# RWKV-7 loops of a hybrid decoder trunk: the second head pair's keys projected in the first loop's filling, the first pair's last transposes behind them

## The chip, the cores and the metric

The kernel runs on 1 core of one Trainium2 chip. The metric is the device time of one execution in microseconds, the median over several executions. The engines are TensorE (PE in the profile, with PEld for its weight loads), VectorE (DVE), ScalarE (ACT), GpSimd (POOL) and SyncE (SP, which issues most DMAs).

## The reference, cut to what matters

One decoder layer on a sequence of 1024 rows of width 1024: three mixers side by side (HGRN2, dilated window attention, RWKV-7) share one input projection `w_in`; then come an output projection, a gated MLP and an embedding term. The change touches the RWKV-7 mixer and the shared projection that fills its gaps:

```python
r, k, v, wd, ad, gd = jnp.split(cm, splits, axis=-1)      # columns of w_in, mixed with the row before
...
kk = heads(k * k_k)
kk = kk / jnp.maximum(jnp.linalg.norm(kk, axis=-1, keepdims=True), 1e-12)
...
def step(state, inp):
    r_t, w_t, k_t, v_t, kk_t, a_t = inp
    sa = jnp.einsum('bhvk,bhk->bhv', state, -kk_t)
    state = (state * w_t[:, :, None, :] + sa[..., None] * (kk_t * a_t)[:, :, None, :]
             + v_t[..., None] * k_t[:, :, None, :])
    return state, jnp.einsum('bhvk,bhk->bhv', state, r_t)
...
mean = jnp.mean(y, axis=-1, keepdims=True)
var = jnp.mean((y - mean) ** 2, axis=-1, keepdims=True)
y = ((y - mean) * lax.rsqrt(var + RK_GN_EPS)).reshape(B_, S_, RK_WIDTH) * ln_w + ln_b
bonus = jnp.sum(rh * kh * r_k, axis=-1, keepdims=True) * vh
y = (y + bonus.reshape(B_, S_, RK_WIDTH)) * g
```

There are 4 heads of 64, treated as two pairs of 128 channels.

## The kernel before, in words

**The projection and its steps.** `w_in` is cut into column blocks of 128. A block `j` is projected as a product of 1024x128 weights and the 1024x1024 input, in float32 by three passes over split operands: `mm3` runs, for each of 8 slices of the contraction, high by high (L137), low by high (L139) and high by low (L141), two halves of 512 columns each. So a *step* is 6 matmuls into the PSUM tile `dp`, and a block is 8 steps, 48 matmuls. There are 2 dp buffers. The weights come by DMA (`wraw`), are cast to their high part on ScalarE (`whi`, L114) and get their low part on POOL or DVE (`wlo`, L116).

Blocks 0 to 7 are RWKV's own columns (2, 3 and 4 the keys k, receptances r and values v of the first pair, 5, 6 and 7 those of the second); `proj` gives `mix_in` a PSUM tile of one, from `self.early` where it is there already, or by computing it in place. A block's result is scaled on DVE (L320), mixed on ScalarE (L501) and on DVE (L502). Blocks from 8 on belong to the other mixers; they have no place of their own in RWKV, and serve as filling.

**The filling.** `project_rest` is a generator over such blocks: each `next(fill)` issues one step on TensorE. A block's end is drained by `finish` (L454 on DVE for blocks that only need scaling, a scaling L320, ScalarE's L457 and DVE's L459 for the others) into the tile `zst` (2 buffers), which SP stores.

**The order of a pair** (`rwkv`, for p in 0, 1). `rwkv_prep` projects k and r, norms the keys (`kks`, L558, sums of squares; the `lo` matmuls L567 and L570), makes `kkn`, `bhat` and `ar` (L594 to L609) on DVE, issues a count of filling steps, and calls `rwkv_scores` (`sc`, L654, masked on DVE, L656). `rwkv_inverse` then inverts the score tiles by 31 rounds on DVE (L678 and L680, with the end L682), to which DMAs bring and from which they take the matrices (`scz` L664, `At` L670, `Tz` and `Uz` L685, `Tc` L690, `Uc` L695). Over that time 32 filling steps are issued in the first pair, 29 in the second, with the projection of v (in the first pair) and the bonus matmuls `bon` (L635) at fixed steps. `rwkv_main` joins the results (`py`, `pu`, `sk`, all by L790) and runs the groups of the scan with one filling step to a slot; a group's outputs `pyo` and states `pS` come by L790, the state S is updated on DVE (L903), and outputs are added to y (L930). `rwkv_norm` norms a half of 512 columns: mean (`gnm`), variance (`gnv`, L760 and L761), its power on POOL (`gnr`, L763), the product on DVE (L764), four transposes `yt` on TensorE (L770), then L771 to L775 on DVE with the gate `pg` (L774). Half 0 is normed within the loop, half 1 behind it. In the first pair the filling is then drained to its end.

A scheduler of the language orders the instructions of each engine by priorities of the code and its model of when each is ready, and gives a tile the buffer that is free first; a buffer asked for must have been read by all its readers.

Of the kernel before, what the change touches and what calls it, by code (L numbers as in the profile page):

```python
# [18 lines left out]
P = 128  # L19
# [70 lines left out]
class Trunk:  # L90
# [334 lines left out]
    def project_rest(self, js):  # L425


        nc = self.nc
        w = None
        for i, j in enumerate(js):  # L430
            w = w or self.load_w(self.a["w_in"][j])
            ps = self.dps.tile([P, T], F32, tag="dp", name=self.nm("dp"))
            nxt = None
            for k in range(ND):
                self.mm3({0: ps[:, :HT], 1: ps[:, HT:]}, w(k), self.X[k], k == 0, k == ND - 1)
                if k == 3 and i + 1 < len(js):
                    nxt = self.load_w(self.a["w_in"][js[i + 1]])
                yield
            w = nxt
            t = self.keep.tile([P, T], F32, tag="zst", name=self.nm("zst"), bufs=2)  # L440
            kind = (j - 8) % 4 if j < 24 else 2
            parts = [(t, ps, self.R)]
            if j < 24 and kind < 3:
                parts = [(t[:, :HT], ps[:, HT:][:, ::-1], self.R[:, HT:][:, ::-1]), (t[:, HT:], ps[:, :HT], self.R[:, :HT])]
            for part in parts:
                self.finish(kind, *part)
            d = self.zpool.tile([P, T], F32, tag=f"z{j}", name=f"z{j}")
            nc.sync.dma_start(d, t)
            self.z[j] = d
        yield  # L450
# [55 lines left out]
    def rwkv(self):  # L506
        nc, tc = self.nc, self.tc
        lt = self.mix_in(0, 6, "lora")
        nc.scalar.activation(lt[0:64, :], lt[0:64, :], AF.Tanh)
        sg = self.mix_in(1, 7, "sg")  # L510
        nc.scalar.activation(sg, sg, AF.Sigmoid)
        self.z = {}
        js = iter((*range(8, 16), 24, 25, 26, 16, 17, 20, 21, 19, 27, 28, 29, 18, 22, 23))
        for p in (0, 1):
            d = {}
            lead, n = self.FILL[p]
            fill = self.project_rest([next(js) for _ in range(n)])
            with tc.tile_pool(name=f"pre{p}", bufs=1) as tp:
                self.rwkv_prep(p, tp, lt, d, fill)
                self.rwkv_inverse(p, tp, d)  # L520
            for i in range(8 * lead - (3 if p else 8)):
                next(fill)
                if p == 0 and i == 1:
                    d["v"] = self.mix_in(4, 4, "v")
                if i == (7 if p else 16):
                    self.rwkv_bonus(d)
            with tc.tile_pool(name=f"rk{p}", bufs=1) as rp:
                self.rwkv_main(p, rp, sg, d, fill)
            self.rwkv_norm(p, sg, d, 1, fill, 6 - 3 * p)
            if p == 0:  # L530
                for _ in fill:
                    pass
        self.rest, self.more = list(js), fill
# [3 lines left out]
    def rwkv_prep(self, p, tp, lt, d, fill):  # L537

        nc, par = self.nc, self.par
# [24 lines left out]
        for hf in (0, 1):  # L564
            sl = slice(hf * HT, (hf + 1) * HT)
            ps = mxp.tile([P, HT], F32, tag="mx", name=self.nm("lo"))
            nc.tensor.matmul(ps, par[0:64, PC_LORA + p * P:PC_LORA + (p + 1) * P], lt[0:64, sl], start=True, stop=True)  # L567
            nc.scalar.activation(w[:, sl], ps, AF.Sigmoid, bias=col(PC_W0))
            ps = mxp.tile([P, HT], F32, tag="mx", name=self.nm("lo"))
# [39 lines left out]
            nc.vector.tensor_tensor(a4[:, :, :, 1:], k4[:, :, :, 1:], g4[:, :, :, :63], ALU.mult)  # L609
            nc.scalar.copy(a4[:, :, :, 0:1], k4[:, :, :, 0:1])  # L610
        d.update(ar=ar, be=be, kh=kh)
        for _ in range(6 if p else 8):
            next(fill)
        self.rwkv_scores(p, tp, d)
        if p:
# [115 lines left out]
    HALVES = tuple((slice(a, a + 32), slice(a + 32, a + 64)) for a in (0, 64))  # L731

    def rwkv_norm(self, p, sg, d, hf, fill, n):
        for i, _ in enumerate(self.rwkv_norm_steps(p, sg, d, hf)):
            for _ in range(2 if i < 4 else 1):
                for _ in range(1 if n == 3 else 2):
                    next(fill, None)

    def rwkv_norm_steps(self, p, sg, d, hf):

        nc, mxp, par = self.nc, self.mxp, self.par
        y, y3 = d["y"], d["y3"]

        def col(c):
            return par[:, c + p:c + p + 1]

        sl, cs = slice(hf * HT, (hf + 1) * HT), slice(8 * hf, 8 * hf + 8)
        y, y3 = y[:, sl], y3[:, cs, :]
        if hf == 0:
            d["o"] = self.keep.tile([P, T], F32, tag="oc", name=self.nm("oc"), bufs=2)  # L750
        o = d["o"][:, sl]
        mean = self.spool.tile([P, 8], F32, tag="kr1", name=self.nm("gnm"), bufs=1)
        nc.vector.tensor_reduce(mean, y3, AX.X, ALU.add)
        nc.vector.tensor_scalar(mean, mean, 1.0 / 64, None, ALU.mult)
        yield
        nc.vector.tensor_tensor(y3, y3, mean.unsqueeze(2).broadcast_to([P, 8, 64]), ALU.subtract)
        nc.scalar.activation(o, y, AF.Square)
        yield
        var = self.spool.tile([P, 8], F32, tag="kr2", name=self.nm("gnv"), bufs=1)
        nc.vector.tensor_reduce(var, o.rearrange("p (c v) -> p c v", v=64), AX.X, ALU.add)  # L760
        nc.vector.tensor_scalar(var, var, 1.0 / 64, GN_EPS, ALU.mult, ALU.add)  # L761
        rs = self.spool.tile([P, 8], F32, tag="kr3", name=self.nm("gnr"), bufs=1)
        nc.gpsimd.tensor_tensor(rs, var, self.mhalf[:, :8], ALU.pow)  # L763
        nc.vector.tensor_tensor(y3, y3, rs.unsqueeze(2).broadcast_to([P, 8, 64]), ALU.mult)  # L764

        yield
        yield
        pt = mxp.tile([P, HT], F32, tag="mx", name=self.nm("yt"))
        for m in range(4):
            nc.tensor.transpose(self.turned(pt[:, m * P:(m + 1) * P], m % 2), y[:, m * P:(m + 1) * P], self.ident)  # L770
        nc.vector.tensor_scalar(o, pt, col(PC_LNW), col(PC_LNB), ALU.mult, ALU.add)  # L771
        nc.vector.tensor_tensor(o, o, d["bv"][:, sl], ALU.add)
        pg = mxp.tile([P, HT], F32, tag="mx", name=self.nm("pg"))
        nc.tensor.matmul(pg, par[:, PC_G2 + p * P:PC_G2 + (p + 1) * P], sg[:, sl], start=True, stop=True)  # L774
        nc.vector.tensor_tensor(o, o, pg, ALU.mult)  # L775
        if hf:
            self.o[6 + p] = d["o"]
            self.dump(f"o{6 + p}", d["o"])
        yield
# [1080 lines left out]
```

## Time and profile before

| what | us |
|---|---|
| median of 3 runs (1404.64 to 1406.29) | 1404.72 |
| the profiled execution | 1404.77 |
| its span, the first to the last instruction | 1403.0 |
| TensorE busy | 1375.7 |
| VectorE busy | 1063.7 |
| ScalarE busy | 611.8 |
| GpSimd busy | 395.5 |

The profile times are from the start of the span. In a timeline row stand the start, the duration of the whole group, the engine, the line, the operation, what it writes and reads, its size and the number of instructions in the group; in brackets the idle time before it and what released it. The first pair's scores are at 77 us, its norm's transposes at 186 and 199.5 us; the second pair's key sums at 214.7, its scores at 238.6. Matmuls overlap: one begins 0.227 us behind the other and lasts longer.

### The profile page before, as it was taken

The page shows a single profiled execution, that of the slowest core. Times are in us where ns is not written, and L with a number is a line of the kernel's source. Part 1 is how long each engine was busy: PE and PEld are TensorE (multiplying, and loading weights), DVE is VectorE, ACT ScalarE, POOL GpSimd, SP SyncE. Part 2 cuts the span into 40 slices and gives each one's busy share as a digit, 9 for nine tenths or more (in the row PEclk, how much of TensorE's full clock was granted, in tenths as well). Part 3 has the DMA queues.
Part 4 walks back from the last instruction along what each step waited for, and adds up shares of the span by engine and source line. Part 5 has one row for each costly group of instructions (what it writes and reads, how often), then busy time and mean ns, then how long its engine had stood idle before and what let it go on. Part 6 is the DMA issues. An engine that isn't in the chain of part 4 may idle for free.

```text
span 1403.0 us, 22344 instructions
## 1 busy us (share of the span) xinstructions
PE 1375.7 (98%) x8644; PEld 1116.5 (80%) x8644; DVE 1063.7 (76%) x1613; ACT 611.8 (44%) x1049; POOL 395.5 (28%) x287
## 2 busy tenths in 40 slices
PE   9999999999999999999999999999999999999997
PEld 6878777877878768788788888888888888888886
DVE  7696456835667796468889888888988799777685
ACT  7522323133255584255544343444344444455542
POOL 5411012101222242221345454545453000002342
PEclk9999999999999999999999999999999999999998
DMA  6123111321622212653232332332324963441443
GB/s 224 61 83 104 64 61 47 100 73 62 225 83 99 91 61 71 253 180 125 94 127 98 113 103 90 102 105 98 114 98 166 351 217 106 127 143 45 136 138 140
DMA packets 80122, 167.61 MB, mean 119 GB/s; under 512 B 19984, under 2 KB 22288, under 8 KB 80016
## 3 DMA queue, kind: packets, MB, share of 16 engines
q1 hardware_dynamic: 66784, 147.05, 31.3%
q10 hardware_dynamic: 12224, 15.47, 3.2%
q0 software_dynamic: 1008, 3.67, 0.7%
q8 instruction: 68, 1.11, 0.3%
q14 instruction: 38, 0.31, 0.1%
HBM read 119.76 MB, written 46.40 MB: 118 GB/s over the span
## 4 chain that ended last, share of the span: by engine, by line
PE 78%; DVE 8%; issue 8%; ACT 3%; POOL 3%; DMA 1%; SPq 0%; POOLq 0%; ACTq 0%; DVEq 0%
PE bg L1338 17%; PE bv L1338 13%; PE bv L1639 7%; PE bg L1639 7%; PE dp L137 7%; PE dp L139 7%; PE dp L141 7%; PE swq L1169 1%; DVE ig L584 1%; PE hsc L1015 1%; PE zp L137 1%; DVE xl L409 1%; PE zp L141 1%; PE zp L139 1%; PE swo L1209 1%
## 5 line engine op out<-in xcount | busy, mean ns | idle before, releaser
L137 PE MATMUL dp<-xh,whi 128*128 128x512 f32 x544 | 186.9, 406 | 1.2 <-DVE r L502 0.7
L139 PE MATMUL dp<-xl,whi 128*128 128x512 f32 x544 | 180.5, 394 | 0.6 <-DVE xl L409 0.5
L141 PE MATMUL dp<-xh,wlo 128*128 128x512 f32 x544 | 179.7, 392 | 0.0
L116 POOL TENSOR_TENSOR wlo<-wraw,whi 128x512 fp32r<-128x512 f32 x60 | 84.5, 1410 | 264.9 <-ACT whi L114 226.8
L116 POOL TENSOR_TENSOR wlo<-raw,whi 128x512 fp32r<-128x512 f32 x84 | 135.0, 1626 | 75.9 <-ACT whi L114 75.9
L114 ACT CAST whi<-wraw 128x512 fp32r<-128x512 f32 x120 | 72.9, 618 | 158.0 <-PE dp L139 103.0
L1338 PE MATMUL bg<-t,whi 128*128 128x512 f32 x352 | 133.4, 389 | 0.0
L139 PEld LDWEIGHTS dp<-xl,whi 128*128 128x128 f32 x544 | 102.3, 188 | 24.6 <-DVE xl L409 2.5
L141 PEld LDWEIGHTS dp<-xh,wlo 128*128 128x128 f32 x544 | 102.2, 188 | 23.8 <-issue 2.0
L137 PEld LDWEIGHTS dp<-xh,whi 128*128 128x128 f32 x544 | 98.8, 189 | 26.0 <-issue 3.9
L116 POOL TENSOR_TENSOR wlo<-s,whi 128x512 fp32r<-128x512 f32 x44 | 64.5, 1466 | 168.6 <-ACT whi L114 168.6
L1639 PE MATMUL bg<-t,whi 128*128 128x512 f32 x308 | 95.2, 390 | 0.0
L1639 PE MATMUL bv<-t,whi 128*128 128x512 f32 x308 | 94.8, 389 | 0.0
L114 ACT CAST whi<-raw 128x512 fp32r<-128x512 f32 x88 | 52.7, 620 | 93.7 <-issue 48.5
L114 ACT CAST whi<-s 128x512 fp32r<-128x512 f32 x66 | 38.9, 620 | 120.2 <-PE bg L1338 112.8
L1338 PEld LDWEIGHTS bg<-t,whi 128*128 128x128 f32 x352 | 66.1, 188 | 13.7
L190 POOL TENSOR_TENSOR rst<-rst,mhalf 128x4 f32<-128x4 f32 (+1 forms) x9 | 10.2, 1134 | 234.0 <-DVE rst L186 218.0
L1635 ACT CAST t<-t 128x512 fp32r<-128x512 f32 x77 | 47.8, 622 | 45.8 <-PE bv L1639 32.7
L1338 PE MATMUL bg<-t,wlo 128*128 128x512 f32 x176 | 67.5, 389 | 0.0
L1639 PEld LDWEIGHTS bv<-t,whi 128*128 128x128 f32 x308 | 57.8, 188 | 12.0
L1639 PEld LDWEIGHTS bg<-t,whi 128*128 128x128 f32 x308 | 57.8, 188 | 11.9
L116 DVE TENSOR_TENSOR wlo<-wraw,whi 128x512 fp32r<-128x512 f32 x60 | 48.2, 807 | 20.7 <-ACT whi L114 18.5
(417 smaller groups left out, 3423.6 us busy)
## 6 DMA issues: line engine op xcount, KB each, us to landing
raw<-in_ffn_up_dram SPq DMA_DIRECT2D x44, 512.0 KB, 3.5
wraw<-in_w_in_dram SPq DMA_DIRECT2D x28, 512.0 KB, 3.4
z<-zst SPq DMA_DIRECT2D x18, 512.0 KB, 2.9
gb<-ct SPq DMA_DIRECT2D x33, 256.0 KB, 2.3
t<-gb SPq DMA_DIRECT2D x33, 256.0 KB, 2.7
t<-gt SPq DMA_DIRECT2D x33, 256.0 KB, 2.7
zl<-z SPq DMA_DIRECT2D x16, 512.0 KB, 4.4
wraw<-in_ple_gate_dram SPq DMA_DIRECT2D x16, 512.0 KB, 3.4
```

The lines of the kernel that those rows point to most:

```text
L114: self.cast = nc.scalar.copy(hi, src).ins
L116: eng.tensor_tensor(lo, src, hi.bitcast(F32), ALU.subtract)
L137: nc.tensor.matmul(ps[hf], wh, xh[hf], start=first, stop=False)
L139: nc.tensor.matmul(ps[hf], wh, xl[hf], start=False, stop=False)
L141: self.step = nc.tensor.matmul(ps[hf], wl, xh[hf], start=False, stop=last).ins
L409: nc.vector.scalar_tensor_tensor(lo, x, g[:, k:k + 1], hi.bitcast(F32), ALU.mult, ALU.subtract)
L584: nc.vector.reciprocal(ig[:, hf * HT:(hf + 1) * HT], gam[:, hf * HT:(hf + 1) * HT])
L1015: nc.tensor.matmul(sc[g:g + 64, c, :], ks[:, c * P + g:c * P + g + 64], x, start=True, stop=True)
L1169: m = nc.tensor.matmul(pq[h][:, b:b + w], d["q"][hs, qb * P:nk], d["k"][hs, b:b + w], start=True, stop=True)
L1338: nc.tensor.matmul(ps, w[part == 2][:, s], X[k][part == 1], start=start and k == part == 0, stop=k == 3 and part == 2, skip_group_check=no ...
L1635: nc.scalar.copy(xh, x)
L1639: nc.tensor.matmul(ps[m], wt[part == 2][:, m * P:(m + 1) * P], (xh, xl)[part == 1], start=k == part == 0, stop=k == NK - 1 and part == 2)
```

## The change

Four edits. `project_rest` accepts a block below 8: it leaves the result in PSUM under `self.early[j]`, where `proj` finds it, and goes on. The first pair's filling gets block 5 as its last, so the second pair's keys are projected in the steps behind the first loop, and no longer in `rwkv_prep`. `rwkv_prep` issues one more step ahead of the scores (9 instead of 8 in the first pair, 7 instead of 6 in the second). And `rwkv_norm` remembers, in the first pair, the instruction of the fifth step that it issues, and the four transposes of half 1 are issued with an order behind it.

```diff
@@ -437,6 +437,9 @@
                     nxt = self.load_w(self.a["w_in"][js[i + 1]])
                 yield
             w = nxt
+            if j < 8:
+                self.early[j] = ps
+                continue
             t = self.keep.tile([P, T], F32, tag="zst", name=self.nm("zst"), bufs=2)
             kind = (j - 8) % 4 if j < 24 else 2
             parts = [(t, ps, self.R)]
@@ -514,7 +517,7 @@
         for p in (0, 1):
             d = {}
             lead, n = self.FILL[p]
-            fill = self.project_rest([next(js) for _ in range(n)])
+            fill = self.project_rest([next(js) for _ in range(n)] + [5] * (p == 0))
             with tc.tile_pool(name=f"pre{p}", bufs=1) as tp:
                 self.rwkv_prep(p, tp, lt, d, fill)
                 self.rwkv_inverse(p, tp, d)
@@ -609,7 +612,7 @@
             nc.vector.tensor_tensor(a4[:, :, :, 1:], k4[:, :, :, 1:], g4[:, :, :, :63], ALU.mult)
             nc.scalar.copy(a4[:, :, :, 0:1], k4[:, :, :, 0:1])
         d.update(ar=ar, be=be, kh=kh)
-        for _ in range(6 if p else 8):
+        for _ in range(7 if p else 9):
             next(fill)
         self.rwkv_scores(p, tp, d)
         if p:
@@ -731,10 +734,15 @@
     HALVES = tuple((slice(a, a + 32), slice(a + 32, a + 64)) for a in (0, 64))
 
     def rwkv_norm(self, p, sg, d, hf, fill, n):
+        steps = 0
+        self.before = None
         for i, _ in enumerate(self.rwkv_norm_steps(p, sg, d, hf)):
             for _ in range(2 if i < 4 else 1):
                 for _ in range(1 if n == 3 else 2):
                     next(fill, None)
+                    steps += 1
+                    if p == 0 and steps == 5:
+                        self.before = self.step
 
     def rwkv_norm_steps(self, p, sg, d, hf):
 
@@ -766,8 +774,11 @@
         yield
         yield
         pt = mxp.tile([P, HT], F32, tag="mx", name=self.nm("yt"))
-        for m in range(4):
-            nc.tensor.transpose(self.turned(pt[:, m * P:(m + 1) * P], m % 2), y[:, m * P:(m + 1) * P], self.ident)
+        with ExitStack() as order:
+            if hf and self.before:
+                order.enter_context(self.tc.issue_after(self.before))
+            for m in range(4):
+                nc.tensor.transpose(self.turned(pt[:, m * P:(m + 1) * P], m % 2), y[:, m * P:(m + 1) * P], self.ident)
         nc.vector.tensor_scalar(o, pt, col(PC_LNW), col(PC_LNB), ALU.mult, ALU.add)
         nc.vector.tensor_tensor(o, o, d["bv"][:, sl], ALU.add)
         pg = mxp.tile([P, HT], F32, tag="mx", name=self.nm("pg"))
```

The line numbers of the rows below are of each kernel's own: those of the changed kernel are 3 higher from L440 on, 8 higher from L745 on and 11 higher from L769 on. The numbers behind a name count the tiles.

**TensorE, behind the first loop.** dp_334 and dp_330 are block 5, the second pair's keys; yt are the transposes of half 1, pg the gate. Before:

```order
L137 MATMUL dp_334_2067<-xh_3_91,whi_329_2059 128x512
L139 MATMUL dp_334_2067<-xl_20_108,whi_329_2059 128x512
L139 MATMUL dp_334_2067<-xl_4_92,whi_329_2059 128x512
L770 MATMUL yt_325_2044<-cst_76,y_190_1155 128x128
L770 MATMUL yt_325_2044<-cst_76,y_190_1155 128x2x64
L770 MATMUL yt_325_2044<-cst_76,y_190_1155 128x128
L770 MATMUL yt_325_2044<-cst_76,y_190_1155 128x2x64
L774 MATMUL pg_326_2051<-sg_83_458,par_75 128x512
L141 MATMUL dp_334_2067<-xh_19_107,wlo_330_2061 128x512
L141 MATMUL dp_334_2067<-xh_3_91,wlo_330_2061 128x512
L137 MATMUL dp_334_2067<-xh_21_109,whi_329_2059 128x512
```

Now:

```order
L139 MATMUL dp_330_2046<-xl_32_120,whi_320_1961 128x512
L139 MATMUL dp_330_2046<-xl_16_104,whi_320_1961 128x512
L141 MATMUL dp_330_2046<-xh_31_119,wlo_321_1963 128x512
L141 MATMUL dp_330_2046<-xh_15_103,wlo_321_1963 128x512
L781 MATMUL yt_333_2103<-cst_76,y_192_1169 128x128
L781 MATMUL yt_333_2103<-cst_76,y_192_1169 128x2x64
L781 MATMUL yt_333_2103<-cst_76,y_192_1169 128x128
L781 MATMUL yt_333_2103<-cst_76,y_192_1169 128x2x64
L785 MATMUL pg_334_2110<-sg_83_458,par_75 128x512
L137 MATMUL dp_357_2171<-xh_17_105,whi_352_2163 128x512
L137 MATMUL dp_357_2171<-xh_1_89,whi_352_2163 128x512
L139 MATMUL dp_357_2171<-xl_18_106,whi_352_2163 128x512
```

The transposes stood behind the first 10 matmuls of the keys; now all 48 stand ahead of them, and dp_357, block 6 (r), follows. Before, 38 matmuls of the keys and 23 of r came between pg and `kks`; now 18 of r do. From kks to the second pair's scores 71 matmuls of dp stood before, and 72 stand now.

**TensorE, behind the second pair's scores.** dp_392 is v (block 7), dp_372 block 24 and dp_404 block 25, bon the bonus matmuls. Before:

```order
L139 MATMUL dp_372_2263<-xl_32_120,whi_370_2259 128x512
L139 MATMUL dp_372_2263<-xl_16_104,whi_370_2259 128x512
L141 MATMUL dp_372_2263<-xh_31_119,wlo_371_2261 128x512
L141 MATMUL dp_372_2263<-xh_15_103,wlo_371_2261 128x512
L635 MATMUL bon_412_2578<-bv_396_2422,cst_76 128x512
L635 MATMUL bon_413_2581<-bv_396_2422,cst_76 128x512
L137 MATMUL dp_404_2531<-xh_17_105,whi_375_2290 128x512
L137 MATMUL dp_404_2531<-xh_1_89,whi_375_2290 128x512
```

Now:

```order
L139 MATMUL dp_392_2367<-xl_32_120,whi_390_2363 128x512
L139 MATMUL dp_392_2367<-xl_16_104,whi_390_2363 128x512
L141 MATMUL dp_392_2367<-xh_31_119,wlo_391_2365 128x512
L141 MATMUL dp_392_2367<-xh_15_103,wlo_391_2365 128x512
L137 MATMUL dp_372_2263<-xh_31_119,whi_370_2259 128x512
L137 MATMUL dp_372_2263<-xh_15_103,whi_370_2259 128x512
L139 MATMUL dp_372_2263<-xl_32_120,whi_370_2259 128x512
L139 MATMUL dp_372_2263<-xl_16_104,whi_370_2259 128x512
L141 MATMUL dp_372_2263<-xh_31_119,wlo_371_2261 128x512
L141 MATMUL dp_372_2263<-xh_15_103,wlo_371_2261 128x512
L137 MATMUL dp_404_2531<-xh_17_105,whi_375_2290 128x512
L137 MATMUL dp_404_2531<-xh_1_89,whi_375_2290 128x512
```

v's last matmuls stood 12 matmuls ahead of the end of block 24, now 6, and the bonus matmuls, which stood between blocks 24 and 25, now follow 42 matmuls of block 25. In the changed kernel dp_404 has the PSUM buffer of dp_372, in the kernel before that of dp_392.

**VectorE, first norm of the first pair.** gnv is the variance, gnr its power, S the state, zst the drain of a filling block. Before:

```order
L760 TENSOR_REDUCE gnv_311_1926<-oc_297_1824 128x8
L903 SCALAR_TENSOR_TENSOR S_292_1806<-pS_293_1807,gC_135_725,N_274_1662 128x64
L761 TENSOR_SCALAR gnv_311_1926<-gnv_311_1926 128x8
L764 TENSOR_TENSOR y_190_1155<-y_190_1155,gnr_312_1929 128x512
L903 SCALAR_TENSOR_TENSOR S_299_1834<-pS_300_1835,gC_135_725,N_274_1662 128x64
L116 TENSOR_TENSOR wlo_356_2169<-wraw_350_2161,whi_355_2167 128x512
```

Now:

```order
L768 TENSOR_REDUCE gnv_311_1932<-oc_297_1830 128x8
L914 SCALAR_TENSOR_TENSOR S_292_1812<-pS_293_1813,gC_137_739,N_274_1668 128x64
L457 TENSOR_TENSOR zst_299_1834<-dp_237_1474,rstd_121 128x512 x2
L769 TENSOR_SCALAR gnv_311_1932<-gnv_311_1932 128x8
L772 TENSOR_TENSOR y_192_1169<-y_192_1169,gnr_312_1935 128x512
L914 SCALAR_TENSOR_TENSOR S_301_1846<-pS_302_1847,gC_137_739,N_274_1668 128x64
```

A drain of two instructions (dp_237, block 14 of the filling) now stands between the variance's sum and its scaling; before, it stood five rows further on. On GpSimd the row behind this gnr is now a weight's low part, `wlo_321`, where a memset (`Uc_402`) stood before.

In the first pair the scores keep their place on TensorE. Behind them stood 39 matmuls of block 9, the bonus and 48 matmuls of v; now come 12 of block 9, 48 of v and 27 of block 9, the bonus 108 rows later, and `py` one step later. On VectorE v's L320 now stands ahead of the first L678 and L502 behind the third; on ScalarE three casts of weights stand ahead of v's L501; on SP the store of block 8 and a weight load stand ahead of the `At` copies. From the middle of the second loop on the two orders agree on TensorE.

## Prediction

> **What bounds the kernel now.** First the page: the busy times, and the chain that ended last.
>
> ```profile
> PE 1375.7 (98%) x8644; PEld 1116.5 (80%) x8644; DVE 1063.7 (76%) x1613; ACT 611.8 (44%) x1049; POOL 395.5 (28%) x287
> ```
>
> TensorE is busy 1375.7 of 1403.0 us. The change adds and removes no matmul, so only TensorE's 27.3 us of idle time can change. The table by windows gives the idle time of the stretch that is edited (columns: window, its length, then PE, PEld, DVE, ACT and POOL busy, clock, DMA share, GB/s):
>
> ```profile
> 60.00:100.00 40.00, 39.03 (x249) 31.25 (x249) 36.30 (x53) 8.98 (x16) 10.06 (x7) 1.00 0.26 86
> 130.00:175.00 45.00, 44.35 (x770) 34.20 (x769) 19.37 (x58) 18.46 (x51) 3.86 (x3) 1.00 0.21 73
> 215.00:240.00 25.00, 23.61 (x190) 18.17 (x189) 18.72 (x17) 9.07 (x13) 5.07 (x3) 1.00 0.06 22
> 275.00:330.00 55.00, 54.52 (x776) 42.35 (x774) 24.38 (x66) 19.16 (x51) 2.58 (x2) 1.00 0.24 69
> ```
>
> Idle: 0.97, 0.65, 1.39 and 0.48, and between them, at 199 us, one wait of 1.65 whose row follows below: together 5.14 us. That is all that the edits can win here. TensorE's waits name the other causes (in all, times, longest):
>
> ```profile
> PE sc L654 <- DVE ar L609: 1.4, 2, 0.8
> PE dp L137 <- DVE r L502: 0.7, 1, 0.7
> PE sk L790 <- DVE S L903: 0.6, 1, 0.6
> ```
>
> The sum is made against the profiled execution, 1404.77 us (span 1403.0 and 1.77 around it), 0.05 above the median of 1404.72. It takes 0.2%, 2.8 us, to tell a change of this kernel from none.
>
> **The transposes of y (edit 4): −1.65.** TensorE's timeline, with the last join of the first pair and the transposes; then two steps of a projection:
>
> ```profile
> 190.30 0.34 PE L790 MATMUL pyo<-S,MG 64*64 64x64 f32 x8
> ...
> 197.25 0.61 PE L139 MATMUL dp<-xl,whi 128*128 128x512 f32 x2
> 199.52 0.63 PE L770 MATMUL yt<-cst,y 128*128 128x128 f32 x4 [1.65 <-DVE y L764]
> 199.98 1.02 PE L774 MATMUL pg<-sg,par 128*128 128x512 f32 x2
> 200.44 1.02 PE L141 MATMUL dp<-xh,wlo 128*128 128x512 f32 x2
> ...
> 209.05 0.62 PE L141 MATMUL dp<-xh,wlo 128*128 128x512 f32 x2
> ...
> 210.41 0.62 PE L141 MATMUL dp<-xh,wlo 128*128 128x512 f32 x2
> ```
>
> Six matmuls, a step, take 210.41 − 209.05 = 1.36 us, 0.227 each. The y chain takes from 190.30 to 199.52, 9.2 us. Before, 28 matmuls (18 and 10) and the pyo block stood in front of the transposes; now 60 do (12 and 48), 13.6 us. The wait of 1.65 ends with 4 us to spare.
>
> **The second pair's scores (edits 2 and 3): −0.23.** The scores wait for `ar`, a chain that begins with `kks`:
>
> ```profile
> 214.72 1.87 PE L558 MATMUL kks<-few,kksq 128*128 128x2 f32 x16
> ...
> 238.55 1.52 PE L654 MATMUL sc<-ar,bhat 64*64 64x64 f32 x64 [0.56 <-DVE ar L609]
> ```
>
> From kks to scores are 23.83 us, in which TensorE idles 1.39 (0.7 for r, 0.56 for the scores and 0.13 smaller). The matmuls of dp between them were 71 (25, 36, 10), and are 72 (30, 42): the step "more" is nearly used up because kks now comes sooner behind the keys' last matmul. One row more covers 0.23 and leaves 1.16, under whichever name.
>
> **The keys' own chain: +0.4.** Behind the keys' last matmul stood 23 matmuls (5.21 us) ahead of kks; now stand the transposes, pg (200.44 − 199.52 = 0.92) and 18 matmuls (4.08): 5.00. What must fit there is this:
>
> ```profile
> 209.70 1.23 DVE L320 TENSOR_TENSOR dp<-dp,rstd 128x1024 f32<-128x1024 f32 x1 [4.55 <-PE dp L141]
> 212.12 1.28 DVE L502 SCALAR_TENSOR_TENSOR k<-dp,par,k 128x1023 f32<-128x1023 f32 x1 [1.19 <-ACT k L501]
> ...
> 200.42 0.80 DVE L771 TENSOR_SCALAR oc<-yt,par 128x512 f32<-128x512 f32 x1
> 201.26 0.69 DVE L772 TENSOR_TENSOR oc<-oc,bv 128x512 f32<-128x512 f32 x1
> ```
>
> ```profile
> 213.44 1.15 ACT L555 ACTIVATE kksq<-k,par 128x1024 f32<-128x1024 f32 x1 [1.35 <-DVE k L502]
> ```
>
> The squares end at 214.59, 0.13 before kks. Now L771 and L772, 1.49 us, stand on DVE between L320 and L502, where 1.19 were idle: +0.30. The chain needs 5.21 − 0.13 + 0.30 = 5.4 and has 5.0: a wait of 0.4 (bounds 0 and 0.5).
>
> **A new wait for a drain: +1.55.** A projection takes one of two dp buffers. Before, the projection of column block 25 (L137) followed the bonus matmuls:
>
> ```profile
> 251.51 1.96 PE L635 MATMUL bon<-bv,cst 128*128 128x512 f32 x4
> ```
>
> ```profile
> 197.63 1.74 DVE L764 TENSOR_TENSOR y<-y,gnr 128x512 f32<-128x512 f32 x1 [0.56 <-POOL gnr L763]
> ...
> 248.95 1.23 DVE L320 TENSOR_TENSOR dp<-dp,rstd 128x1024 f32<-128x1024 f32 x1 [5.60 <-PE dp L141]
> ...
> 252.57 1.21 DVE L454 TENSOR_TENSOR zst<-dp,rstd 128x1024 f32<-128x1024 f32 x1
> ```
>
> Before, v ended two steps (12 matmuls) ahead of block 24, and block 25 took v's buffer after the bonus. Now v ends one step ahead of 24, the bonus has moved 42 matmuls back, and block 25 takes the buffer of 24, whose only reader is L454. DVE begins 0.19 behind a block's last matmul (the keys' ended at 214.72 − 5.21 = 209.51, L320 began at 209.70). L320 of v takes 1.23 of the step of 1.36, so L454 begins 0.19 behind block 24's last matmul and lasts 1.21. From the end of a DVE row to TensorE's next were 0.15 (L764 ended at 197.63 + 1.74 = 199.37, the transposes began at 199.52). Block 25 waits 0.19 + 1.21 + 0.15 = 1.55 (bounds 1.3 and 1.7). The later of two nearly simultaneous ends is drained with nothing of TensorE's beside it. The Trainium skill ("Perfetto Trace Analysis", section "Matmuls") says that independent groups should rotate through PSUM banks so that draining one overlaps the next group's matmuls. Block 25 breaks that rule here; by the rule the price is a whole drain, 1.21 by the row above, and the sum 0.34 lower.
>
> **The end of the first loop: +0.5.** DVE's rows at the first pair's first norm, POOL's beside its second (whose L764 is shown above), and the join on TensorE:
>
> ```profile
> 178.91 0.69 DVE L764 TENSOR_TENSOR y<-y,gnr 128x512 f32<-128x512 f32 x1 [1.76 <-POOL gnr L763]
> 179.52 0.28 DVE L903 SCALAR_TENSOR_TENSOR S<-pS,gC,N 128x64 f32<-128x64 f32 x1
> ...
> 181.80 1.28 DVE L454 TENSOR_TENSOR zst<-dp,rstd 128x512 f32<-128x512 f32 x2
> ```
>
> ```profile
> 197.56 1.27 POOL L116 TENSOR_TENSOR wlo<-wraw,whi 128x512 fp32r<-128x512 f32 x1
> ```
>
> ```profile
> 181.38 0.34 PE L790 MATMUL pyo<-S,MG 64*64 64x64 f32 x8
> ```
>
> Two things now delay the first norm's L764 and with it the state update L903 behind it: the two L454 stand ahead of gnv (L761), 1.28 us, and POOL starts a wlo right behind gnr, as it did in the second norm, where L764 took 1.74 instead of 0.69: +1.05. Together 2.3. From L903's end (179.80) to the pyo that reads S (181.38) are 1.58: pyo would wait 0.7. DVE idled 1.76 just there before, and part of an L454 may fit into such a gap, so I take 0.5 (bounds 0 and 1.1). The Trainium skill ("SBUF — State Buffer", section "Who interferes with whom") says that a VectorE instruction with two SBUF inputs against a GpSimd one that reads SBUF blocks for the whole instruction, whoever issues first winning. That speaks against this change: by it L764 would last 1.27 − 0.07 + 0.69 = 1.9, an estimate from its rule and these rows, and the term would be 0.15 larger. The 1.74 measured is near it.
>
> **Smaller terms: −0.3 and −0.4.** The `sk` wait on S (0.65, the idle time of the window 130 to 175) comes from S queued on DVE behind a projection's drain; the drains come one step earlier now. Bounds −0.65 and 0; I take the half, −0.3. In the second pair's join TensorE idles 0.48, mostly for the inverse's transposed blocks Tc; the join comes later by the drain's wait and 10 matmuls, and the inverse on DVE by under a us: −0.4 (bounds −0.48 and 0).
>
> **Costed at nothing.** The first pair's scores have the same matmul places: their wait stays.
>
> ```profile
> 77.00 1.52 PE L654 MATMUL sc<-ar,bhat 64*64 64x64 f32 x64 [0.83 <-DVE ar L609]
> ```
>
> Behind them v is projected at once, and on DVE its L320 (1.23) goes ahead of the inverse (L678), whose first row was ready at 89.61:
>
> ```profile
> 89.61 1.29 DVE L678 TENSOR_TENSOR Tt<-At,Tb 64x31 f32<-64x31 f32 x1
> ...
> 122.61 1.12 DVE L682 COPY Ub<-Tb 64x1024 f32<-64x1024 f32 x1
> ```
>
> ```profile
> 132.82 1.20 PE L790 MATMUL py<-Tc,sc 32*32 32x32 f32 x64
> ```
>
> v ends 60 matmuls behind the scores, at 78.5 + 13.6 = 92.1, L320 at 93.5: the inverse starts 3.9 later, and one L320 of the same shape, 1.2, that stood inside it goes, so it ends 2.7 later. py is 1.36 later. In the first pair 10.2 us lie between L682 and py with no wait, in which the Tc copies go out. The tile's own rows give their first and last start, and the time to landing:
>
> ```profile
> L690 SPq DMA_DIRECT2D Tc<-Tz x4: 334/510/682, 125.6 to 127.2; - x4
> ...
> DMA to landing us min/median/max: 1.9/2.9/4.1
> ```
>
> The last is issued at 127.2 and lands 1.9 to 4.1 later, so 1.5 to 3.7 are spare ahead of py, and 1.36 more: 2.9 at least against 2.7. Hidden, just; bounds 0 and +0.5. SP's queue, which the z store of block 8 and one weight load now pass ahead of the At copies, lies in the same slack.
>
> **Sum.** −1.65 − 0.23 + 0.4 + 1.55 + 0.5 − 0.3 − 0.4 = −0.13: 1404.77 − 0.13 = 1404.6 us. An exchange of waits.
>
> **Rivals.** *Faster:* the two new waits and the keys' one don't appear, because DVE runs L454 in a gap. Then −0.13 − 2.45 = −2.58: 1402.2; and if the scores' 1.16 goes too, 1401.0. For it: DVE is idle often. Against it: L454 cannot start before the last matmul of its block. *Slower:* the first pair's v is held on ScalarE. Casts of weights now stand ahead of v's activation (L501):
>
> ```profile
> 94.39 0.62 ACT L114 CAST whi<-wraw 128x512 fp32r<-128x512 f32 x1 [2.25 <-PE dp L139]
> ...
> 103.58 1.12 ACT L501 ACTIVATE v<-dp,omm 128x1024 f32<-128x1024 f32 x1 [3.06 <-DVE dp L320]
> ```
>
> A cast waits for TensorE to release a weight buffer. If they wait for the second weight half of block 9, last read about 85 matmuls behind the scores (97.8), v is ready at 97.8 + 2 × 0.62 + 1.12 = 100.2 instead of 94.6, and DVE's L502, queued three rows into the inverse, holds it 5.6 longer. With 2.7 that is 8.3 against a slack of 2.9 to 5.1: about 4.3 over, 1408.9. It decides above a hold of about 2. Against it: the buffers that those casts take were read by the weights before. *The moved tail:* L771, L772 and L775 (2.2 us) lie wholly on the keys' chain, not 0.3 of them: 1404.6 + 1.9 = 1406.5. Against it: DVE is idle for r's and k's activations there. *It does not do what it says:* the step ahead of scores is already one row in my sum, so this is no case of its own.
>
> **How the numbers follow.** Exchange 0.60, faster 0.20 (half of it, 0.11 with the tails of the others, beyond 2.8 us), moved tail 0.11, slower 0.09. The exchange's own bounds, few of them at once, give about 1403.2 to 1406.0. The range takes in the first step of the faster rival and the moved tail: 1402.2 to 1406.9. Faster by over 0.2% 0.11, within 0.80, slower 0.09.
>
> **What would show it.** Right: no wait at yt; block 25's first L137 waits about 1.55 for L454; a pyo in the first loop's last group waits for S; the second scores wait in all about 1.2; kks waits a few tenths. Wrong: block 25 starts at once, or py of the first pair waits for Tc, or a wait above 1 us anywhere else before 420 us.

## The result and the profile after

| | before | changed |
|---|---|---|
| median of 22 runs, us | 1405.73 (1403.96 to 1406.87) | 1407.92 (1405.47 to 1409.55) |
| ratio, 95% interval | | 1.0013 (1.0007 to 1.0019) |
| profiled execution, us (span) | 1404.77 (1403.0) | 1406.55 (1404.7) |

The change costs 1.8 us (1.0 to 2.7) by the ratio, which goes by the means, 1405.63 and 1407.49; the medians lie 2.2 apart. That is under the 0.2% named in the prediction, and it is clear of zero: not an exchange of waits, as predicted, but a small loss.

TensorE's waits in the changed kernel between 60 and 420 us (in all, times, longest) show that most of the named waits went as predicted:

```profile
PE sc L657 <- DVE ar L612: 2.4, 3, 1.3
PE dp L137 <- DVE zst L457: 1.3, 1, 1.3
PE sk L801 <- DVE S L914: 0.6, 1, 0.6
PE pyo L801 <- DVE S L914: 0.4, 1, 0.4
```

The transposes no longer appear. The projection of block 25 waits for the drain of block 24, and a pyo waits for the state, both forecast. The same in TensorE's timeline:

```profile
184.01 0.33 PE L801 MATMUL pyo<-S,MG 64*64 64x64 f32 x4
184.73 0.27 PE L801 MATMUL pyo<-S,MG 64*64 64x64 f32 x2 [0.39 <-DVE S L914]
...
208.74 0.60 PE L781 MATMUL yt<-cst,y 128*128 128x128 f32 x4
...
214.14 1.84 PE L561 MATMUL kks<-few,kksq 128*128 128x2 f32 x16
...
237.89 0.34 PE L657 MATMUL sc<-ar,bhat 64*64 64x64 f32 x8 [1.30 <-DVE ar L612]
238.48 1.04 PE L657 MATMUL sc<-ar,bhat 64*64 64x64 f32 x56 [0.25 <-DVE ar L612]
...
253.32 0.74 PE L137 MATMUL dp<-xh,whi 128*128 128x512 f32 x2 [1.32 <-DVE zst L457]
```

The transposes begin with no wait; kks follows them by 5.40 us with no wait; the scores still wait, now in two pieces, 1.30 and 0.25. By windows (PE busy of each window's length):

```profile
130.00:175.00 45.00, 44.92 (x753) 1.00 0.27 78
175.00:200.00 25.00, 24.40 (x288) 1.00 0.19 66
215.00:240.00 25.00, 23.45 (x187) 1.00 0.07 23
252.00:275.00 23.00, 21.68 (x92) 1.00 0.27 92
275.00:330.00 55.00, 54.86 (x723) 1.00 0.26 69
330.00:345.00 15.00, 14.25 (x262) 1.00 0.31 107
```

The idle times are 0.08, 0.60, 1.55, 1.32, 0.14 and 0.75, with 0.98 in 60 to 100 5.4 us, as before. And yet the stretch is longer. A wait that the profile brackets is shorter than what it costs: a projection matmul starts 0.227 behind the one ahead but is drawn 0.39 long, and the end drawn hides the first part of every stall. For block 25 the bracket says 1.32, while from the start of block 24's last matmul to the start of its own are 1.70, a stall of 1.47. A break within a join can carry no bracket at all, as that of the first pair's does (below).

A count without this fault compares the starts of the same matmul in both traces and takes off 0.227 for each projection matmul more or less ahead of it. Against the first profile of before the changed kernel loses 0.25 behind the first scores, 0.5 in the first pair's join and 1.1 at the end of the first loop; it wins 0.6 at the first loop's sk and 1.8 at the transposes; it wins 0.2 up to the second scores, loses 1.6 up to the bonus matmuls, wins 0.6 at the second join, and loses 0.4 in the second loop: 0.8 in all, before the parts are rounded. Behind the loops 0.9 more is lost; that is under e5.

### The profile page after: what moved, and what is told of

It reads as the page before. It is cut to its first block, busy times and chain, and to the rows that moved or that the text cites. A ratio compares the mean times of both kernels' runs of the same rounds, so it can differ in the third digit from the quotient of the medians.

```text
span 1404.7 us, 22342 instructions
## 1 busy us (share of the span) xinstructions
PE 1375.7 (98%) x8644; PEld 1116.1 (79%) x8644; DVE 1060.9 (76%) x1613; ACT 612.2 (44%) x1049; POOL 394.5 (28%) x287
## 4 chain that ended last, share of the span: by engine, by line
PE 81%; DVE 9%; issue 3%; ACT 2%; POOL 2%; DMA 2%; SPq 0%; POOLq 0%; ACTq 0%; DVEq 0%
PE bg L1349 17%; PE bv L1349 13%; PE bv L1650 7%; PE bg L1650 7%; PE dp L137 7%; PE dp L139 7%; PE dp L141 7%; PE swq L1180 1%; PE hsc L1026 1%; DVE ig L587 1%; DVE Tt L681 1%; PE zp L137 1%; PE swt L1206 1%; PE swo L1220 1%; PE zp L141 1%
## 5 line engine op out<-in xcount | busy, mean ns | idle before, releaser
L1647 DVE TENSOR_TENSOR t<-t,t 128x512 fp32r<-128x512 f32 x77 | 55.0, 714 | 9.0 <-ACT t L1646 8.7
```

Source lines behind the costliest of these rows:

```text
L1647: V.tensor_tensor(xl, x, xh.bitcast(F32), ALU.subtract)
```

## The experiments

Each stands against runs of the kernel before on the same chip; microseconds are the ratio times 1405. The last column comes from the profiles alone: the time from the first pair's scores to the row of `swd` (L204, a matmul of another mixer at 463 us, behind both loops), less the 385.7 that the two profiles of before took (385.78 and 385.65; the changed kernel 386.56, e4 386.49). Two profiles of the same order differ by about 0.1 there, where a ratio is uncertain by 0.8 to 1.7 us. It leaves out the start, and what comes behind 463 us. The row of swd in the first profile of before and in the changed kernel (the scores of these two begin at 77.00 and 78.01):

```profile
462.78 1.09 PE L204 MATMUL swd<-cst,sden 128*64 128x128 f32 x16
```

```profile
464.57 1.09 PE L204 MATMUL swd<-cst,sden 128*64 128x128 f32 x16
```

| kernel | steps ahead of scores | keys in the filling | ratio (95%) | us | scores to `swd`, us |
|---|---|---|---|---|---|
| changed | 9, 7 | yes | 1.0013 (1.0007 to 1.0019) | +1.8 | +0.8 |
| e4, edit 4 undone | 9, 7 | yes | 1.0014 (1.0005 to 1.0023) | +2.0 | +0.8 |
| e1 | 8, 7 | yes | 0.9999 (0.9991 to 1.0008) | −0.1 | −0.6 |
| e2 | 9, 6 | yes | 0.9993 (0.9984 to 1.0002) | −1.0 | −1.1 |
| e8 | 8, 6 | yes | 0.9982 (0.9973 to 0.9991) | −2.5 | −2.6 |
| e3 | 8, 8 | yes | 0.9971 (0.9959 to 0.9983) | −4.1 | −3.7 |
| e10 | 9, 8 | yes | 0.9982 (0.9973 to 0.9991) | −2.5 | −3.2 |
| e11 | 8, 9 | yes | 0.9966 (0.9954 to 0.9978) | −4.8 | −3.6 |
| e9, low parts on DVE | 9, 7 | yes | 1.0001 (0.9992 to 1.0010) | +0.1 | +0.2 |
| e7 | 9, 7 | no | 1.0018 (1.0009 to 1.0027) | +2.5 | +2.3 |
| e6 | 8, 8 | no | 0.9992 (0.9983 to 1.0001) | −1.1 | −1.5 |
| e5, before again | 8, 6 | no | 1.0002 (0.9993 to 1.0012) | +0.3 | −0.1 |

**e4: the order of the transposes taken away.**

```diff
-            if hf and self.before:
+            if False:
                 order.enter_context(self.tc.issue_after(self.before))
```

> The changed kernel without edit 4 (the transposes have no order behind the fifth step). The order of the instructions on every engine is then the same as in the changed kernel, so edit 4 decides nothing once the keys are in the filling, and this run is a second look at the changed kernel: +1.8 against the kernel before within 0.6. It tells what of the first profile is not of the change: if the inputs at the start land as late as there (+1.2 at 20 us against the kernel before) the start is part of the change, if not it is scatter of one execution.

Measured +2.0 with the same waits in the same places. The order of instructions on all engines is the same without edit 4: once the keys are in the filling, their 48 matmuls stand ahead of the transposes anyway. Edit 4 does nothing.

**e5: the kernel before, a second profile.**

> The kernel before, unchanged, as a second profile of it. All five profiles with the change have the first matmuls 0.9 to 1.4 us later at 20 us than the one profile of before, though the program is the same up to there. If that is scatter of one execution, this profile is late too, by about 1; if it is due to the change, this profile is as the first. Times: 0 within 0.7.

The first pair's scores, ahead of which the programs issue the same, in the changed kernel, in e5, in e1 and in e10:

```profile
78.01 1.52 PE L657 MATMUL sc<-ar,bhat 64*64 64x64 f32 x64 [0.85 <-DVE ar L612]
```

```profile
77.75 1.52 PE L654 MATMUL sc<-ar,bhat 64*64 64x64 f32 x64 [0.83 <-DVE ar L609]
```

```profile
78.37 1.52 PE L657 MATMUL sc<-ar,bhat 64*64 64x64 f32 x64 [0.82 <-DVE ar L612]
```

```profile
77.24 1.52 PE L657 MATMUL sc<-ar,bhat 64*64 64x64 f32 x64 [0.82 <-DVE ar L612]
```

Before had 77.00. The unchanged program has 77.75 here, and among all profiles they lie between 77.0 and 78.4 with no relation to the change. The start is scatter, and the first profile of before was a lucky one there. So the rival "the loss is at the start" falls, though 1.0 of the 1.7 between the first two spans does come from there.

Behind 500 us the first profile was unlucky: TensorE was granted half its clock for some 3.4 us at 511 us (0.50 in the window 511.4 to 514.7), in e5, the changed kernel and e4 not. The first profile of before, e5 and the changed kernel (the column behind PE's is the granted clock):

```profile
500.00:520.00 20.00, 17.56 (x138) 0.91 0.14 41
500.00:520.00 20.00, 17.61 (x167) 1.00 0.14 42
500.00:520.00 20.00, 17.57 (x163) 1.00 0.21 63
```

From swd to the last matmuls (`bv`, L196) the first profile took 933.2 and e5 932.2, so the half clock cost 1.0, and only e5 is a fair measure of what lies behind it. The changed kernel took 932.6, e4 932.5, 0.3 more than e5: at 538 us `vt` waits 1.46 for DVE's `ho`, in e5 1.18. From bv to the end of the span both took 7.6, and e5 7.0. With the 0.8 up to swd this makes 1.7 to 1.8, the time that was measured. The 0.8 is the one counted place by place above. Why the 0.9 behind it is lost is open; e9, with the same steps and keys, has neither part (932.2 and 7.0), so it need not come from the change.

**e1, e2 and e8: one step ahead of the scores undone, then both.**

```diff
-        for _ in range(7 if p else 9):
+        for _ in range(7 if p else 8):     # e1
+        for _ in range(6 if p else 9):     # e2
+        for _ in range(6 if p else 8):     # e8
```

> The changed kernel with the first pair's step ahead of scores undone (8 and 7 instead of 9 and 7). Theory: the changed kernel loses 1.8 us to the one before. Its own profile shows +1.5 for the drain of block 24, -1.8 for the transposes, -0.6 in the second pair's join, and in the first pair +0.4 in the join and +1.1 at the outputs of the last group of the first loop, -0.6 at sk. If the last three come from the first pair's extra step, this run is 0.9 faster than the changed kernel, so about +0.9 against the kernel before, and the wait for block 24's drain stays at 1.3 to 1.6. Rival: the 1.8 come from the start of the program (inputs landing 1 us later in the profile of after) or from the stretch behind 420 us, and then this run is at +1.8 within 0.5, like every other kernel with the change.

> The changed kernel with the second pair's step ahead of scores undone (9 and 6). Theory: the bonus matmuls stand between blocks 24 and 25 again and block 25 no longer waits for the drain of block 24 (-1.5), but the second scores come a step earlier and wait about 1.4 more: near the changed kernel, +1.8 against the kernel before, within 0.5. The wait of dp for zst is gone and that of sc for ar is about 3. Rival: the drain's wait is paid elsewhere anyway and the step is pure gain: this run is 1.4 slower than the changed kernel, +3.2.

> The changed kernel with both steps undone (8 and 6): the keys in the filling alone. Theory: the transposes' wait goes (-1.65), block 25 stands behind the bonus matmuls and waits for no drain, the scores of the second pair wait as long as before or 0.5 less: -1.9 against the kernel before by the profiles, -3 if the times of the runs with one step undone add up. Rival: the saved wait comes back at the second scores, which hang on the keys: 0.

Both steps cost: −0.1 and −1.0 against the +1.8 of the changed kernel, so e1 gains 1.9 where I expected 0.9. Without either the kernel is 2.5 faster than before, between the 1.9 and the 3 expected. The costs add up: by the times the first pair's ninth step costs 1.9 (e1 to the changed kernel) and 1.5 (e8 to e2), the second pair's seventh 2.4 (e8 to e1) and 2.8 (e2 to the changed kernel), each uncertain by 1.5 to 1.8. The profiles up to swd give 1.45 twice for the ninth step and 2.0 twice for the seventh. My expectation for e2 was wrong by nearly 3 us: I held that the scores would wait 1.4 more with a step less. TensorE in e2:

```profile
214.18 1.85 PE L561 MATMUL kks<-few,kksq 128*128 128x2 f32 x16
...
237.93 1.52 PE L657 MATMUL sc<-ar,bhat 64*64 64x64 f32 x64 [1.33 <-DVE ar L612]
...
252.27 1.96 PE L638 MATMUL bon<-bv,cst 128*128 128x512 f32 x4
```

From kks to scores are 23.75 us in e2, and 23.75 in the changed kernel, and the wait is 1.33 against 1.30. The step did not come ahead of the scores at all: with 6 steps the scheduler puts 5 matmuls of v there instead, 71 in place of 72. What the step does is to shift block 24 by six matmuls against v, and with it the drain: in e2 and e8 block 25 follows the bonus matmuls and waits for nothing. With the wait of sk for S in the second loop (idle in 330 to 345: 0.75 in the changed kernel, 0.20 in e2) the drain's 1.47 makes 2.0, the step's cost by the profiles. The break of 0.25 in the scores costs 0.1 from start to start.

The idle time of e1 at the end of the first loop and in the second:

```profile
175.00:200.00 25.00, 25.00 (x284) 1.00 0.19 66
...
252.00:275.00 23.00, 22.77 (x96) 1.00 0.26 92
...
330.00:345.00 15.00, 14.27 (x264) 1.00 0.30 107
```

With 8 steps in the first pair no pyo waits (25.00 busy); the second pair's sk keeps its 0.73. (The window 252 to 275 cuts block 25's wait at its start, in e1 at 250.9.)

**e3: a step more in the second pair, not less.**

```diff
-        for _ in range(7 if p else 9):
+        for _ in range(8):
```

> The changed kernel with 8 steps ahead of the scores in both pairs (instead of 9 and 7). In the second pair block 24 then ends ahead of the scores and is drained beside them, and v's 48 matmuls come between it and block 25. Theory: no wait of dp for zst (-1.5), the second scores wait 0.2 to 0.3 instead of 1.6 (-1.3), and the first pair is as in the kernel with 8 and 7 (-0.9): together -3.7 against the changed kernel, about -1.9 against the kernel before. Rival: the later scores make the second inverse late and the time comes back at the join: py waits 1.4 for Tc, and the run is at -0.5 against the kernel before. Rival of the place: the 1.8 don't come from this stretch, and the run is at -1.0 or above.

Measured −4.1, which is 5.9 below the changed kernel where 3.7 were expected: the direction and the place are right, and both steps cost more than the profiles' rows had told. To swd it is 4.5 below the changed kernel. The windows of e3:

```profile
215.00:240.00 25.00, 24.75 (x190) 1.00 0.07 23
252.00:275.00 23.00, 23.00 (x100) 1.00 0.18 67
275.00:330.00 55.00, 54.92 (x797) 1.00 0.26 78
```

78 matmuls cover the second scores, whose wait falls from 1.55 to 0.25; block 24 ends ahead of them and its drain has v's 48 matmuls beside it; and the join waits for nothing, so the time does not come back there. The saved us stay saved.

**e10 and e11: 9 and 8, 8 and 9.**

> The changed kernel with 9 and 8 steps. Theory: the first pair's ninth step costs by itself, in its join and in its last group, whatever the second pair does: 1.4 to 2.0 more than with 8 and 8, so about -2.4 against the kernel before. Rival: it costs only beside the second pair's 7: as with 8 and 8, -4.1.

> The changed kernel with 8 and 9 steps: six more matmuls of a further block ahead of the second scores. Theory: with 8 the scores have 0.25 of wait left, so a ninth step gains 0.25 at most, and it puts one step of block 25 ahead of v, so that v ends with block 25 half open: the next block waits for v's buffer, whose last reader is v's L505, 1.2 to 2.5 of new wait: -2 to -3 against the kernel before. Rival: more steps ahead of the scores are better still: below -4.1.

e10 lands on its number, −2.5, but does not show what it was made for: the 1.6 by which it stands above e3 are uncertain by 2.1, and to swd the two profiles differ by 0.5 alone. The ninth step costs 1.5 there up to the second scores, but e3 gives most of the rest back in the second loop, where TensorE idles 0.40 between 330 and 345 us in e3 and not at all in e10. e11 was forecast wrongly. The wait that I named, of a block for v's buffer, does not appear; another does, v itself waits for block 24's drain behind the scores:

```profile
237.17 1.16 PE L657 MATMUL sc<-ar,bhat 64*64 64x64 f32 x64
239.85 0.74 PE L137 MATMUL dp<-xh,whi 128*128 128x512 f32 x2 [1.52 <-DVE zst L457]
```

That 1.5 takes what the ninth step wins at the scores and further on, and e11 and e3 are equal: within their intervals, and to 0.1 at swd. Both are faster than the kernel before and the changed one.

**e6 and e7: the steps without the keys.** The kernel before with the counts of e3, and of the changed kernel.

```diff
-        for _ in range(6 if p else 8):
+        for _ in range(8):                 # e6
+        for _ in range(7 if p else 9):     # e7
```

> The kernel before with 8 steps ahead of the scores in both pairs, and the keys not in the filling. Theory: the transposes wait their 1.65 again and r its 0.7, the second scores are covered by 73 matmuls instead of 71 (-0.45), no drain is waited for, and the join comes later (-0.5): -1.0 against the kernel before. Against the kernel with the change and 8 and 8 (measured at -4.1) that is +3. Rival: the two steps are what made that kernel fast and the keys in the filling are worth nothing: this run is at -3 to -4.

> The kernel before with edit 3 alone (9 and 7). Theory: the first pair's step costs 1.4 to 2 and the second pair's 1.6 to 2.9, as between the runs before, and the transposes still wait 1.65, less 0.9 for four matmuls more ahead of them: together +2 to +4 against the kernel before, slower than the changed kernel. Rival: the steps cost only together with the keys in the filling: 0.

Both as expected, −1.1 and +2.5. The keys in the filling are worth 2.5 with 8 and 6 steps, 3.0 with 8 and 8, but 0.7 with 9 and 7 by the times; 2.6, 2.2 and 1.4 by the profiles up to swd. With 9 and 7 the first loop's end lies in the way: from start to start it costs e7 0.4 and the changed kernel 1.1. In e7 no low part stands on POOL behind gnr, the first norm's product takes 0.69, and no pyo waits for S, though the two drains stand ahead of gnv there as well. The transposes wait 1.5 again, and the drain's wait is there too. DVE at the first norm, then TensorE:

```profile
179.12 1.28 DVE L454 TENSOR_TENSOR zst<-dp,rstd 128x512 f32<-128x512 f32 x2
180.32 0.16 DVE L761 TENSOR_SCALAR gnv<-gnv 128x8 f32<-128x8 f32 x1
...
182.61 0.69 DVE L764 TENSOR_TENSOR y<-y,gnr 128x512 f32<-128x512 f32 x1 [1.53 <-POOL gnr L763]
```

```profile
201.54 0.63 PE L770 MATMUL yt<-cst,y 128*128 128x128 f32 x4 [1.54 <-DVE y L764]
...
239.67 1.52 PE L654 MATMUL sc<-ar,bhat 64*64 64x64 f32 x64 [1.61 <-DVE ar L609]
254.06 0.72 PE L137 MATMUL dp<-xh,whi 128*128 128x512 f32 x2 [1.32 <-DVE zst L454]
```

**e9: no low part on POOL behind the first norm.** The low parts of the weights of blocks 5 and 6 are all made on DVE.

```diff
-    def load_w(self, src):
+    def load_w(self, src, own=None):
...
-            parts.append(self.split2(raw[:, b * HT:(b + 1) * HT], self.nc.gpsimd if self.uid % 2 else self.nc.vector))
+            parts.append(self.split2(raw[:, b * HT:(b + 1) * HT], own or (self.nc.gpsimd if self.uid % 2 else self.nc.vector)))
...
-                    nxt = self.load_w(self.a["w_in"][js[i + 1]])
+                    nxt = self.load_w(self.a["w_in"][js[i + 1]], nc.vector if js[i + 1] == 5 else None)
...
-            w = self.load_w(self.a["w_in"][j])
+            w = self.load_w(self.a["w_in"][j], self.nc.vector if j == 6 else None)
```

> The changed kernel with the low parts of the weights of blocks 5 and 6 all made on VectorE, so that no low part follows the first norm's gnr on POOL; on TensorE the order stays. Theory: the product of the norm on DVE lasts 0.69 instead of 1.77 there, the state update behind it comes 1.1 earlier, and the outputs of the last group no longer wait for it (0.4 and the 0.2 behind it): the profile loses 0.6 to 1.0 in that place, against the changed kernel, at about +1.0 against the kernel before. Rival: the two drains ahead of gnv are the delay that counts, and DVE's two low parts more take the place of the hold: the wait for S stays over 0.3 and the time at +1.8.

DVE and POOL at the first norm in the changed kernel:

```profile
179.40 0.28 DVE L914 SCALAR_TENSOR_TENSOR S<-pS,gC,N 128x64 f32<-128x64 f32 x1
179.59 1.28 DVE L457 TENSOR_TENSOR zst<-dp,rstd 128x512 f32<-128x512 f32 x2
180.79 0.16 DVE L769 TENSOR_SCALAR gnv<-gnv 128x8 f32<-128x8 f32 x1
182.71 1.77 DVE L772 TENSOR_TENSOR y<-y,gnr 128x512 f32<-128x512 f32 x1 [1.76 <-POOL gnr L771]
184.41 0.27 DVE L914 SCALAR_TENSOR_TENSOR S<-pS,gC,N 128x64 f32<-128x64 f32 x1
```

```profile
181.03 1.64 POOL L771 TENSOR_TENSOR gnr<-gnv,mhalf 128x8 f32<-128x8 f32 x1 [0.18 <-DVE gnv L769]
182.63 2.98 POOL L116 TENSOR_TENSOR wlo<-wraw,whi 128x512 fp32r<-128x512 f32 x2
```

And DVE in e9:

```profile
182.21 0.69 DVE L772 TENSOR_TENSOR y<-y,gnr 128x512 f32<-128x512 f32 x1 [1.76 <-POOL gnr L771]
182.82 0.28 DVE L914 SCALAR_TENSOR_TENSOR S<-pS,gC,N 128x64 f32<-128x64 f32 x1
...
184.50 1.88 DVE L116 TENSOR_TENSOR wlo<-wraw,whi 128x512 fp32r<-128x512 f32 x3
```

The product takes 0.69 instead of 1.77, the state comes 1.1 earlier behind it, and the pyo's wait is gone. In its place pS waits 0.5 for the next state, so that of the 1.1 only 0.5 is left at the transposes, start to start: half of the rival came true. To swd e9 is 0.7 below the changed kernel. The time is +0.1, 1.7 below it; the two intervals allow 0.2 to 3.2. The hold by POOL is shown, and its worth in the time is 0.7 by the profile, by the times only its sign.

## Why the prediction was wrong

The forecast was −0.1 and 1404.6; measured are +1.8 and 1407.9. 1.0 of the miss in the absolute time is the kernel before itself: 22 runs of it have a median of 1405.73, where the three that the forecast started from had 1404.72. The rest is the sum, step by step:

- *The transposes, −1.65:* right. No wait, −1.8 from start to start. But it was put down to edit 4, and that edit is inert (e4): the keys in the filling do it.
- *The second scores, −0.23:* the reasoning was right that the step is nearly used up, and the wait stayed: idle 1.39 before, 1.55 after in that window. Start to start it is −0.2. The cover was never the point of that step, as e2 shows.
- *The keys' own chain, +0.4:* wrong, 0. I took 0.92 for the transposes and pg from the starts of grouped rows; from the transposes to kks are 5.40, where I had 5.00. The chain of 5.4 just fits.
- *The drain of block 24, +1.55:* right, 1.47 from start to start. e2, e8 and e3 take it away, in two different ways.
- *The end of the first loop, +0.5:* right in mechanism, and too small: 1.1. L772 took 1.77, as the second norm's row had told, and all of the two drains' 1.28 lay ahead of it; no gap took them up. The working gave 0.7 and I cut it to 0.5. pyo's break, 0.2 for MG and a broken order of pyo and pS stand behind it. The Trainium skill's rule ("SBUF — State Buffer", section "Who interferes with whom"), by which the forecast estimated 1.9, is near the 1.77: POOL began at 182.63, DVE at 182.71, and without POOL's row the same instruction took 0.69 (e9, and e7).
- *sk, −0.3:* the wait in the first loop went (−0.6), but the same wait came in the second loop, 0.4 to 0.55: sum near 0. The second loop's filling is shifted by the second pair's step in the same way, and I did not carry the reason over to it. In e1 both loops have it, in e2 neither.
- *The second join, −0.4:* right, −0.6.
- *The first join, costed at nothing:* wrong, +0.5. I looked for Tc to be late, and Tc was not. TensorE in the changed kernel, then ScalarE in the kernel before and in the changed one:

```profile
139.02 0.24 PE L801 MATMUL pu<-Uc,Y 32*32 32x32 f32 x2
139.19 0.44 PE L801 MATMUL sk<-ar,khat 64*64 64x128 f32 x4
139.56 1.19 PE L801 MATMUL pu<-Uc,Y 32*32 32x32 f32 x62
```

```profile
135.76 0.58 ACT L720 COPY Y<-py 32x512 f32<-32x512 f32 x1
136.36 0.60 ACT L457 ACTIVATE zst<-dp 128x512 f32<-128x512 f32 x1
```

```profile
138.28 0.62 ACT L460 ACTIVATE zst<-dp 128x512 f32<-128x512 f32 x1
138.92 0.58 ACT L723 COPY Y<-py 32x512 f32<-32x512 f32 x1
```

The filling's drain, shifted by the step, stood behind the second copy of Y on ScalarE and now stands ahead of it; pu begins, breaks and goes on when Y is whole. No wait is bracketed, since sk's matmuls fill part of the break.

With the measured sizes the sum is −1.8 − 0.2 + 0 + 1.6 + 1.1 − 0.6 + 0.4 − 0.6 + 0.5 + 0.25 = +0.65, or +0.8 before rounding, as counted directly up to swd. The 0.25 is at v's projection behind the first scores, and was not in the forecast; in e1, e3 and e8, without the ninth step, it is not there. The rest up to 1.8 are the 0.9 behind swd, of which only the place is known (e5), and where the forecast had priced nothing.

Of the rivals, *slower* was named with the wrong mechanism: v was not held on ScalarE, its activation began at 94.96, 0.04 behind L320's end. The moved tail of the norm cost nothing.

The failed step of the working is the price of the first pair's ninth step. The forecast put it at +0.5 at the end of the loop and −0.3 at sk, +0.2 in all; it measured +1.45 up to swd (e1 to the changed kernel). Three sizes were wrong: the end of the first loop cost 1.1 for 0.5, the first join 0.5 where only Tc had been looked at, and v's projection 0.25 where nothing had been looked for. The second pair's step brought back in the second loop what sk had won in the first. That the sum up to swd missed by no more than 0.9 is luck in part, since the keys' 0.4 erred the other way. Behind all of it is one omission: the extra steps were treated as small shifts with each wait priced alone, and they moved every drain of the filling by one step through both loops.

## What to carry to other kernels

A filling that is moved by one step moves all its drains, and these stand on the same queues as the work that they fill: walk through every loop behind it, and not only the place of the edit. Judge a number of steps by what the scheduler really puts ahead of the waiting instruction: here one step bought one matmul, the next bought six. And where two edits are made together, price them apart: the keys in the filling won 2.5 us, the steps chosen with them lost 4.3 by the times and 3.4 by the profiles, and two other choices of the counts end 4 to 5 below the kernel before by the times, 3.6 and 3.7 by the profiles.

## What was not expected of the hardware

The start of the program scatters nearly as much as the whole effect: in 13 profiles the first pair's scores, reached by the same instructions, began between 77.0 and 78.4 us. In the changed kernel the first weights landed 0.9 later than in the first profile of before (their cast to the high part began at 4.72 against 3.86), and in e5, the kernel before, 0.8 later. Two profiles of two kernels are thus compared from a common place inside.

The granted clock scatters too, and it has to be looked at before two profiles are compared. In 5 of the 13 (before, e3, e6, e7 and e11) TensorE had half its clock for some 3.4 us between 508 and 518 us. In the first profile of before this came behind a wait of 2.44 us (`vt` for ScalarE's `hV`), but e5 has the same wait, 2.39, and kept the full clock. Over the 33 runs of the kernel before beside e5 the time goes with the mean granted clock: 1404.3 us on average at 0.996, 1405.3 at 0.995 and 1405.7 at 0.994.

And the bracketed idle times of TensorE were equal (5.4 us each) in stretches that differ by 0.8 us.
